# Opening of an encoder layer: the fourth chunk's low weight part moved from a transfer to VectorE, two casts placed later

## The chip, the cores and the metric

One Trainium2 chip, one of its cores. The metric is the device time of one execution in microseconds (us), the median over the runs. The engines are called by their short names in the rows: PE is TensorE (PEld its weight loads), DVE is VectorE, ACT is ScalarE, POOL is GpSimd, and SP is the queue from which most transfers are issued.

## The reference

The kernel computes one layer of a bidirectional encoder on 512 tokens with 1024 channels, in float32. Three sub-layers add to the residual stream: a SwiGLU feed-forward, a mixer of two attentions, and a second SwiGLU. Each begins with an RMS norm that is modulated by a shift and a scale, and these come from a conditioning vector:

```python
c_act = jax.nn.silu(c)
mod = c_act @ w_mod[l] + b_mod[l]
(sh1, sc1, g1, sh2, sc2, g2, sh3, sc3, g3) = jnp.split(mod, N_MOD, axis=-1)
h = modulate(rmsnorm(x, norm_ffn1[l]), sh1, sc1)       # h * (1 + scale) + shift
x = x + 0.5 * g1[:, None, :] * swiglu(h, w_ffn1_in[l], w_ffn1_out[l])
```

Only the start of the first SwiGLU, `h @ w_ffn1_in` for the first four column pairs, matters here.

## The kernel before

Float32 products are made from rounded parts. A number is written as `high + low`, where `high` is the value rounded to the format `float32r` and `low` is the rest. A product is the sum of three matmuls: high by high, high by low and low by high.

The opening computes the first 1024 columns of `h @ w_ffn1_in` (four gate and four up blocks of 128). It goes through the 1024 channels in eight **chunks** `k` of 128. All eight accumulators (`out1`) stay in PSUM, and each chunk adds 24 matmuls of 512 columns: eight of `wh` by `hh[k]`, eight of `wh` by `hl[k]`, eight of `wl` by `hh[k]`. For chunk 7 they are grouped by two accumulators, so `wl` is used after the first four matmuls there. Matmuls of a chunk can't begin before that chunk's `hh` and `wh` are made.

For each chunk this is prepared:

- **Transfers** (`first_loads`): 512 KB of `w_mod` for the scale (`SC1`), 512 KB of the weights (`w1s` into a `raw` tile), 512 KB of `w_mod` for the shift (`SH1`). SP issues them in this order, three chunks ahead; from chunk 3 on each waits until the older tile in its buffer is used up.
- **Scale and shift** (`mod_col`, L282): DVE reduces each 128x1024 tile of `w_mod` against the conditioning vector to a column. For the scale a short ACT instruction (L291) finishes the column.
- **Scaling** (`scaled`, L680): DVE multiplies the chunk of `x` by the inverse root, one 128x512 instruction, made a chunk ahead.
- **Rounding** (`first_high`): ACT applies scale and shift with output `hh[k]` rounded (L692, 128x512), and again unrounded in two halves (L695). DVE subtracts these (`low()`, L699, two halves) to get `hl[k]`.
- **Weights' high part**: ACT casts `raw` to `high` (L668, "the cast").
- **Weights' low part**: for the chunks not in `BY_DMA`, DVE subtracts `raw - high` (`first_low`, L674). For the chunks in `BY_DMA`, ACT writes `low = -raw` rounded (L666), and a GpSimd transfer adds the exact weights from memory to it (L667): what is left is weight minus rounded weight. This transfer reads the same 512 KB again.

The high and low weight parts go round five buffer slots, and `raw` has five buffers. In this part of the program each engine runs its instructions in the order in which the code writes them (`manual_schedule`), so a waiting instruction holds up all that stands behind it on its engine. The order is set by the loop over `k` below: in turn `k` come `first_high(k)`, the cast of chunk `k+1`, for a `BY_DMA` chunk the preparation of chunk `k+2`, the loads of `k+3`, and the DVE work.

After the opening the rest of the layer follows on PE without any other change between the two programs.

Of the kernel before, what the change touches and what calls it, by code (L numbers as in the profile page):

```python
# [14 lines left out]
AF = mybir.ActivationFunctionType  # L15
ALU = mybir.AluOpType
# [104 lines left out]

LAST = 2

BY_DMA = (3, 5, 7)

TO_MIX = (4, 13, 2, 2, 4, 2, 1)
TO_FFN2 = (3, 1, 2, 2, 3, 2, 1)
# [6 lines left out]
def layer(ctx: ExitStack, tc: tile.TileContext, a: dict):  # L134
    nc = tc.nc
    V, S, G, PE = nc.vector, nc.scalar, nc.gpsimd, nc.tensor
# [32 lines left out]
    def f(ap):  # L169
        return ap.bitcast(F32)  # L170
# [25 lines left out]
    def high_low(n=1024, aside=0, holder=None):  # L196
        while turn[0] % HILO in holders:
            turn[0] += 1
        i = turn[0] % HILO
        turn[0] += 1  # L200
        if holder:
            holders[i] = holder
        i = i * (1024 + GAP) + ASIDE + aside
        return tuple(t[:, i : i + n] for t in parts)
# [41 lines left out]
    def mod_load(v, c, w=None, n=1):  # L246
        if w is None:
            w = u4(F32).rearrange("p a b -> p (a b)")
        load_by(w, a["w_mod"][v * NC + c], n)
        return w  # L250
# [22 lines left out]
    def mod_col(v, c, w=None, in_order=False, beside=False, n=1):  # L273
        if w is None:
            w = mod_load(v, c)
        t, b = modv[v][:, c : c + 1], mod_begin(v)[:, c : c + 1]
        by = 1.0 if v in norms or v in (SH1, SH2, SH3) else -0.5 if v == G3 and c % 4 < 2 else 0.5
        so_far = 0.0 if v in norms else b
        for i in range(n):
            j = slice(i * 1024 // n, (i + 1) * 1024 // n)  # L280
            total = t if i == n - 1 else small(1)
            ins = V.tensor_tensor_reduce(  # L282
                out=w[:, j], in0=w[:, j], in1=cact[0][:, j], scale=by, scalar=so_far, op0=ALU.mult, op1=ALU.add,
                accum_out=total,
            )
            so_far = total
        if in_order:
            tc.keep_in_program_order(ins)
        if v in norms:
            if beside:  # L290
                S.activation(t, t, AF.Identity, bias=b, scale=par[:, norms[v] + c : norms[v] + c + 1])  # L291
            else:
                V.scalar_tensor_tensor(t, t, par[:, norms[v] + c : norms[v] + c + 1], b, ALU.mult, ALU.add)
# [332 lines left out]
    with tc.manual_schedule(engines=BOUND | {mybir.EngineType.SP, mybir.EngineType.Pool}):  # L626
# [22 lines left out]
        w1, kept = {}, []  # L649

        def first_loads(k):
            n = 1 if k else 2
            scale = mod_load(SC1, k, n=n)
            if k == 0:
                kept.append(keep([P, 2 * NC], "pos", I32)[:, 0:NT])
            shift = mod_load(SH1, k, n=n) if k == 0 else None
            raw = sbuf("raw", [P, 1024], F32, RAW)
            load_by(raw, a["w1s"][k], n)
            w1[k] = [scale, shift or mod_load(SH1, k), raw]

        def first_split(k):

            raw = w1[k][2]
            hi, lo = high_low()
            if k in BY_DMA:
                S.activation(lo, raw, AF.Identity, scale=-1.0)  # L666
                G.dma_start(lo, a["w1s"][k], accum_op=ALU.add)  # L667
            S.copy(hi, raw)  # L668
            w1[k] += [hi, lo]

        def first_low(k):
            raw, hi, lo = w1[k][2:]
            if k not in BY_DMA:
                V.tensor_tensor(lo, raw, f(hi), ALU.subtract)  # L674

        def scaled(k, rb=None, r=FULL[0]):
            if k not in scaled_x:
                scaled_x[k] = f2()
            rb = spread_sb if rb is None else rb
            V.tensor_tensor(scaled_x[k][:, r], x[k][:, r], rb, ALU.mult)  # L680

        def first_high(k, parts=FULL, between=lambda r: None):

            t = scaled_x.pop(k)
            if k % 4 == 0:
                values = b8(F32).rearrange("p a b -> p (a b)")
                for i in range(2):
                    hq[f"b{k // 4 + 1}{i + 1}"] = values[:, i * 1024 : (i + 1) * 1024]
            v = [hq[f"b{k // 4 + 1}{n + 1}"][:, k % 4 * H : (k % 4 + 1) * H] for n in range(2)]
            by = {"bias": modv[SH1][:, k : k + 1], "scale": modv[SC1][:, k : k + 1]}  # L690
            for r in parts:
                S.activation(hh[k][:, r], t[:, r], AF.Identity, **by)  # L692
                between(r)
            for u, r in zip(v, HALVES):
                S.activation(u, t[:, r], AF.Identity, **by)  # L695

            def low():
                for u, r in zip(v, HALVES):
                    V.tensor_tensor(hl[k][:, r], u, f(hh[k][:, r]), ALU.subtract)  # L699

            return low

        def first_products(k, outs, w, h, r, first, last):
            for i in outs:
                PE.matmul(
                    out1[i][:, r], w[:, i * P : (i + 1) * P], h[:, r],
                    start=first and r.start == 0, stop=last and r.stop == T, skip_group_check=True,
                )
# [60 lines left out]
        raw = w1[0][2]  # L769
# [25 lines left out]
        low()  # L795
        scaled(1)
        first_split(1)
        out1 += [bank("op"), bank("tp")]
        first_products(0, range(6, 8), wh, hh[0], FULL[0], True, False)
# [5 lines left out]
        for k in range(1, NC):  # L805
            low = first_high(k)
            if k + 1 < NC:
                if k + 1 not in BY_DMA:
                    first_split(k + 1)
                if k + 2 in BY_DMA:  # L810
                    first_split(k + 2)
                if k + 3 < NC:
                    first_loads(k + 3)
                scaled(k + 1)
                if k in BY_DMA:
                    mod_col(SC1, k + 1, w1[k + 1][0], beside=True)
                first_low(k)
                low()
                if k not in BY_DMA:
                    mod_col(SC1, k + 1, w1[k + 1][0], beside=True)  # L820
                mod_col(SH1, k + 1, w1[k + 1][1])
            else:
                low()
                first_low(k)
            wh, wl = w1.pop(k)[3:]
            groups = [range(2 * i, 2 * i + 2) for i in range(4)] if k == NC - 1 else [every]
            for outs in groups:
                for w, h in ((wh, hh[k]), (wh, hl[k]), (wl, hh[k])):
                    first_products(k, outs, w, h, FULL[0], False, k == NC - 1 and w is wl)
# [253 lines left out]
    for i in range(2):  # L1083
# [3 lines left out]
            scale=1.0, scalar=0.0, op0=ALU.mult, op1=ALU.add, accum_out=lam_s[:, i : i + 1],  # L1087
# [1021 lines left out]
```

## Time and profile before

| what | value |
|---|---|
| median of 3 runs | 1037.63 us (1037.6 to 1039.89) |
| the profiled execution | 1036.79 us |
| its span, first to last instruction | 1035.0 us |
| PE busy over the span | 1028.5 us (99%) |
| DVE, ACT, POOL busy | 787.0, 583.8, 163.2 us |
| PE idle in the opening's chunks, 20 to 60 us | 1.3 us, once |
| granted TensorE clock, mean | 0.999 |
| data moved by transfers | 220.92 MB |

In the rows that follow, a timeline row has the start in us from the span's begin, the duration in us, the engine, the line and operation, what is written and read, and in brackets the engine's idle time before it with what ended the wait. A row of the chain of waits has start, duration and the engine and line that the end of the program hung on at that time. A row of instruction groups has busy time, the mean of one in ns, and idle time before them. A row of transfers has the count, the size of each and the us from issue to landing. Lines (L...) are those of the program before.

### The profile page before, as it was taken

The numbers are of one execution on the slowest core, as the hardware profiler recorded it, in microseconds if no ns is written. First come the engines' busy times: TensorE is split into PE (matmuls) and PEld (weight loads), VectorE is DVE, ScalarE is ACT, GpSimd is POOL, SyncE is SP. The second block draws the span as 40 slices with busy tenths as digits, with TensorE's granted clock in tenths as the row PEclk, the third lists the DMA queues.
The fourth block names the chain that finished last, engine by engine and source line by source line (L and its number), as shares of the span: only waits on it lengthen the run. The fifth ranks groups of instructions, "written<-read, shape, count | busy, mean of one in ns | idle before, by whom it ended". The sixth has DMA issues, their size and how long they took to land.

```text
span 1035.0 us, 18850 instructions
## 1 busy us (share of the span) xinstructions
PE 1028.5 (99%) x7346; PEld 949.4 (92%) x7346; DVE 787.0 (76%) x1456; ACT 583.8 (56%) x1014; POOL 163.2 (16%) x190
## 2 busy tenths in 40 slices
PE   9999999999999999999999999999999999999998
PEld 7789899899998998899888888989999999999998
DVE  7787667567797679859772598976899777877877
ACT  6664335244365343668785856525867546654553
POOL 1101110110110100543333101001112112112210
PEclk9999999999999999999999999999999999999999
DMA  9977887966884459796737944974498998999974
GB/s 359 359 239 203 233 231 214 255 167 209 250 204 137 149 197 410 242 285 136 187 74 189 252 138 154 363 255 101 92 238 194 237 227 219 221 227 216 209 156 112
DMA packets 70377, 220.92 MB, mean 213 GB/s; under 512 B 8464, under 2 KB 13200, under 8 KB 70288
## 3 DMA queue, kind: packets, MB, share of 16 engines
q1 hardware_dynamic: 47808, 146.52, 39.2%
q0 software_dynamic: 19344, 68.70, 36.1%
q10 hardware_dynamic: 3136, 4.51, 1.2%
q8 instruction: 57, 0.93, 0.3%
q14 instruction: 32, 0.26, 0.1%
HBM read 209.46 MB, written 10.23 MB: 212 GB/s over the span
## 4 chain that ended last, share of the span: by engine, by line
PE 95%; DMA 2%; DVE 1%; ACT 1%; issue 0%; SPq 0%; DVEq 0%; ACTq 0%
PE acc L458 7%; PE acc L457 7%; PE acc L459 7%; PE sc L459 6%; PE sc L458 6%; PE sc L457 6%; PE sc L173 5%; PE sc L174 5%; PE sc L175 5%; PE acc L173 5%; PE acc L175 5%; PE acc L174 5%; PE tp L1277 2%; PE sc L186 2%; DMA raw<-w1s 2%; PE acc L1198 2%
## 5 line engine op out<-in xcount | busy, mean ns | idle before, releaser
L189 ACT CAST high<-raw 128x1024 fp32r<-128x1024 f32 (+2 forms) x176 | 158.4, 914 | 152.2 <-PE sc L174 44.7
L189 DVE TENSOR_TENSOR low<-raw,high 128x1024 fp32r<-128x1024 f32 (+2 forms) x176 | 183.1, 1050 | 41.2 <-ACT high L189 36.6
L457 PE MATMUL acc<-b,high 128*128 128x256 f32 x508 | 140.8, 277 | 0.0
L458 PE MATMUL acc<-b,high 128*128 128x256 f32 x508 | 140.6, 277 | 0.1
L459 PE MATMUL acc<-b,low 128*128 128x256 f32 x508 | 140.5, 277 | 0.0
L459 PE MATMUL sc<-b,low 128*128 128x256 f32 x500 | 138.2, 276 | 0.0
L457 PE MATMUL sc<-b,high 128*128 128x256 f32 x500 | 138.2, 276 | 0.0
L458 PE MATMUL sc<-b,high 128*128 128x256 f32 x500 | 138.2, 276 | 0.0
L189 ACT CAST high<-u 128x1024 fp32r<-128x1024 f32 (+1 forms) x73 | 75.5, 1034 | 50.6 <-PE sc L174 20.0
L189 DVE TENSOR_TENSOR low<-u,high 128x1024 fp32r<-128x1024 f32 (+1 forms) x73 | 87.6, 1200 | 20.6 <-ACT high L189 19.1
L173 PE MATMUL sc<-b,high 128*128 128x512 f32 (+1 forms) x272 | 97.4, 358 | 0.0
L174 PE MATMUL sc<-b,high 128*128 128x512 f32 (+1 forms) x272 | 97.0, 357 | 0.0
L175 PE MATMUL sc<-b,low 128*128 128x512 f32 (+1 forms) x272 | 97.0, 357 | 0.0
L458 PEld LDWEIGHTS acc<-b,high 128*128 128x128 f32 x508 | 95.5, 188 | 0.4 <-DVE b L1893 0.3
L457 PEld LDWEIGHTS acc<-b,high 128*128 128x128 f32 x508 | 95.4, 188 | 0.3 <-ACT f L535 0.2
L459 PEld LDWEIGHTS acc<-b,low 128*128 128x128 f32 x508 | 95.4, 188 | 0.0
L457 PEld LDWEIGHTS sc<-b,high 128*128 128x128 f32 x500 | 94.0, 188 | 0.0
L458 PEld LDWEIGHTS sc<-b,high 128*128 128x128 f32 x500 | 93.9, 188 | 0.0
L459 PEld LDWEIGHTS sc<-b,low 128*128 128x128 f32 x500 | 93.9, 188 | 0.0
L173 PE MATMUL acc<-b,high 128*128 128x512 f32 (+1 forms) x240 | 89.1, 371 | 0.0
L175 PE MATMUL acc<-b,low 128*128 128x512 f32 (+1 forms) x240 | 86.5, 360 | 0.0
L174 PE MATMUL acc<-b,high 128*128 128x512 f32 (+1 forms) x240 | 86.5, 360 | 0.0
(397 smaller groups left out, 2715.6 us busy)
## 6 DMA issues: line engine op xcount, KB each, us to landing
u<-w_mod SPq DMA_DIRECT2D x38, 512.0 KB, 8.3
b<-w_mod SPq DMA_DIRECT2D x32, 512.0 KB, 5.3
raw<-w2i SPq DMA_DIRECT2D x31, 512.0 KB, 5.6
u<-w2i POOLq DMA_DIRECT2D x31, 512.0 KB, 7.1
raw<-w1u SPq DMA_DIRECT2D x24, 512.0 KB, 5.9
u<-w1u POOLq DMA_DIRECT2D x24, 512.0 KB, 6.9
raw<-w1o SPq DMA_DIRECT2D x24, 384.0 KB, 5.0
raw<-w_gate SPq DMA_DIRECT2D x16, 512.0 KB, 5.2
```

Of the source, the lines that this page charges most:

```text
L173: PE.matmul(out, wh, xh, start=first, stop=False)
L174: PE.matmul(out, wh, xl, start=False, stop=False)
L175: PE.matmul(out, wl, xh, start=False, stop=last)
L186: last = PE.matmul(out, of[j][a], of[j][b], start=i == 0, stop=i == 2).ins
L189: last = S.copy(hi, src), V.tensor_tensor(lo, src, f(hi), ALU.subtract)
L457: PE.matmul(out, wh[:, s], xh, start=first and j == 0, stop=False, skip_group_check=True)
L458: PE.matmul(out, wh[:, s], xl, start=False, stop=False, skip_group_check=True)
L459: PE.matmul(out, wl[:, s], xh, start=False, stop=last and j == 1, skip_group_check=True)
L1198: PE.matmul(out[t][:, 0:n], hh[k][:, ht], wh[:, o : o + n], start=k == 0, stop=False)
L1277: PE.transpose(tp[:, j * P : (j + 1) * P], src, ident)
```

## The change

Chunk 3 leaves `BY_DMA`: its low part is now made by DVE like that of chunks 1, 2, 4 and 6. For the chunks that stay, 5 and 7, the old function is cut in two. `first_minus` (the negated weights and the adding transfer) stays where the whole was, in turn `k-2`; the cast goes to turn `k-1`, as for all other chunks. Since the place of `mod_col(SC1, k + 1)` also hangs on `BY_DMA`, in turn 3 DVE now reduces the scale of chunk 4 after `low()`, not before it.

```diff
-BY_DMA = (3, 5, 7)
+BY_DMA = (5, 7)
...
+        def first_minus(k):
+
+            w1[k] += high_low()
+            raw, _, lo = w1[k][2:]
+            S.activation(lo, raw, AF.Identity, scale=-1.0)
+            G.dma_start(lo, a["w1s"][k], accum_op=ALU.add)
+
         def first_split(k):
 
-            raw = w1[k][2]
-            hi, lo = high_low()
-            if k in BY_DMA:
-                S.activation(lo, raw, AF.Identity, scale=-1.0)
-                G.dma_start(lo, a["w1s"][k], accum_op=ALU.add)
-            S.copy(hi, raw)
-            w1[k] += [hi, lo]
+            if k not in BY_DMA:
+                w1[k] += high_low()
+            S.copy(w1[k][3], w1[k][2])
...
             if k + 1 < NC:
-                if k + 1 not in BY_DMA:
-                    first_split(k + 1)
+                first_split(k + 1)
                 if k + 2 in BY_DMA:
-                    first_split(k + 2)
+                    first_minus(k + 2)
```

How the order on the engines changes is shown at three places. The rows give the line, the operation, what is written and read, and the shape; `raw_151`, `raw_279` and `raw_332`/`raw_334` are the weights of chunks 2, 3 and 5, `b_12_97` and `b_13_98` hold `hh` of chunks 0 to 3 and 4 to 7. The lines of the changed program stand two or three higher from L674 on (L692 is L695 there).

First ACT, around the rounding of chunk 2 (`f_61`), before:

```order
L668 CAST high<-raw_151 128x1024
L666 ACTIVATE low<-raw_279 128x1024
L668 CAST high<-raw_279 128x1024
L291 ACTIVATE mod_89<-mod_89,begin,par 128x1
L692 ACTIVATE b_12_97<-f_61_297,mod_88,mod_89 128x512
L695 ACTIVATE b_45_224<-f_61_297,mod_88,mod_89 128x256 x2
```

and now:

```order
L672 CAST high<-raw_151 128x1024
L291 ACTIVATE mod_89<-mod_89,begin,par 128x1
L695 ACTIVATE b_12_97<-f_61_294,mod_88,mod_89 128x512
L698 ACTIVATE b_45_224<-f_61_294,mod_88,mod_89 128x256 x2
L672 CAST high<-raw_279 128x1024
```

The negation of chunk 3's weights is gone and their cast stands behind chunk 2's scale and rounding.

Second ACT, around the rounding of chunk 4 (`f_69`), where chunk 5's weights are prepared, before:

```order
L666 ACTIVATE low<-raw_334 128x1024
L668 CAST high<-raw_334 128x1024
L291 ACTIVATE mod_89<-mod_89,begin,par 128x1
L692 ACTIVATE b_13_98<-f_69_383,mod_88,mod_89 128x512
L695 ACTIVATE b_70_414<-f_69_383,mod_88,mod_89 128x256 x2
```

and now:

```order
L665 ACTIVATE low<-raw_332 128x1024
L291 ACTIVATE mod_89<-mod_89,begin,par 128x1
L695 ACTIVATE b_13_98<-f_69_380,mod_88,mod_89 128x512
L698 ACTIVATE b_70_412<-f_69_380,mod_88,mod_89 128x256 x2
L672 CAST high<-raw_332 128x1024
```

The negation stays ahead of the rounding, the cast goes behind it. The same holds for chunk 7's weights around the rounding of chunk 6.

Third DVE, in turn 3, before:

```order
L680 TENSOR_TENSOR f_69_383<-x_82,f_44_223 128x512
L282 ISA u_58_291,mod_89<-u_58_291,ka_96 128x1024
L282 ISA mod_89 128x1
L699 TENSOR_TENSOR b_14_99<-b_45_224,b_12_97 128x256 x2
L282 ISA u_60_295,mod_88<-u_60_295,ka_96,par 128x1024
```

and now:

```order
L683 TENSOR_TENSOR f_69_380<-x_82,f_44_223 128x512
L677 TENSOR_TENSOR low<-raw_279,high 128x1024
L702 TENSOR_TENSOR b_14_99<-b_45_224,b_12_97 128x256 x2
L282 ISA u_58_288,mod_89<-u_58_288,ka_96 128x1024
L282 ISA mod_89 128x1
L282 ISA u_60_292,mod_88<-u_60_292,ka_96,par 128x1024
```

One subtraction of 128x1024 is added, and the reduction of chunk 4's scale stands behind chunk 3's `hl`. GpSimd has one adding transfer fewer; PE and SP run the same instructions in the same order.

## The prediction

> **What bounds the kernel now.** I read the page's busy times first, then the waits of PE, then the chain of waits in the opening, then the timelines of PE, ACT and DVE around the place it names, and last the transfers. The busy times and PE's waits from 20 to 60 us:
>
> ```profile
> PE 1028.5 (99%) x7346; PEld 949.4 (92%) x7346; DVE 787.0 (76%) x1456; ACT 583.8 (56%) x1014; POOL 163.2 (16%) x190
> PE acc L705 <- ACT b L692: 1.3, 1, 1.3
> ```
>
> PE fills the span, so only time in which PE stands still can be won without removing matmuls, and the change removes none. In the chunks it stands still once, for 1.3 us, waiting for ACT's rounded chunk. The chain of waits up to that place, then PE's timeline across it:
>
> ```profile
> 13.76 10.60 DMA raw<-w1s
> 24.41 0.94 issue
> 25.36 1.03 ACT high L668
> 26.38 0.30 ACT mod L291
> 26.70 0.82 ACT b L692
> 27.57 0.50 PE acc L705
> ...
> 25.88 0.39 PE L705 MATMUL tp<-b,low 128*128 128x512 f32 x1
> 27.57 0.50 PE L705 MATMUL acc<-b,high 128*128 128x512 f32 x1 [1.30 <-ACT b L692]
> 27.91 0.40 PE L705 MATMUL sc<-b,high 128*128 128x512 f32 x1
> ```
>
> The first matmul of chunk 2 (27.57) hangs on ACT's rounding of chunk 2 (26.70), this on the cast of chunk 3's weights (25.36), and this on the negation ahead of it, which waited for the landing of those weights. The next ACT rows show that wait, and DVE's say when chunk 2's own inputs were there:
>
> ```profile
> 24.39 1.06 ACT L666 ACTIVATE low<-raw 128x1024 fp32r<-128x1024 f32 x1 [2.02 <-DMA raw<-w1s]
> ...
> 24.21 0.07 DVE L282 DVE_READ_ACCUMULATOR2_ANT mod<- 128x1 f32 x1
> 24.82 1.21 DVE L674 TENSOR_TENSOR low<-raw,high 128x1024 fp32r<-128x1024 f32 x1
> 28.04 0.92 DVE L699 TENSOR_TENSOR b<-b,b 128x256 fp32r<-128x256 f32 x2 [2.02 <-ACT b L695]
> ```
>
> The shift of chunk 2, the last input of its rounding, was ready at 24.28. So ACT rounded 2.4 us late, held up by work for the chunk after.
>
> **Part 1: chunk 3's negation and cast leave the front of the queue.** ACT then begins chunk 2's rounding at about 24.28 + 0.09 = 24.37 (0.09 is an estimate of the hand-over; from ACT to PE it is 26.70 + 0.82 to 27.57, 0.05) and ends it 0.82 later, at 25.2. PE's last matmul of chunk 1 starts at 25.88 and the rows are 0.23 apart, so chunk 2 would begin at 26.11 with its weight load one pitch before, at 25.9. The rounding is 0.7 us early: the wait is gone altogether. The gain is read at the second matmul, since the first one after the wait was also longer: without a wait it starts at 25.88 + 2 x 0.23 = 26.34, against 27.91. **Gain: 1.57 us**, made of the 1.3 of idle time and 0.27 of restart.
>
> **Part 2: what chunk 3 now costs.** The cast (1.03) moves behind L695 of chunk 2, to about 26.1; its weights landed at 24.36, and PE wants it at 31.6 (a chunk is 24 x 0.227 = 5.44 us). It costs nothing there. The subtraction joins DVE's turn 3. A full turn on DVE, from the groups between 20 and 60 us:
>
> ```profile
> L282 DVE CUSTOM_DVE_ANT_0 u<-u,ka,par 128x1024 f32<-128x1024 f32 x6 | 7.7, 1277 | 0.0
> L282 DVE CUSTOM_DVE_ANT_0 u<-u,ka 128x1024 f32<-128x1024 f32 x6 | 7.3, 1217 | 0.0
> L699 DVE TENSOR_TENSOR b<-b,b 128x256 fp32r<-128x256 f32 x14 | 5.7, 421 | 6.7 <-ACT b L695 6.4
> L674 DVE TENSOR_TENSOR low<-raw,high 128x1024 fp32r<-128x1024 f32 x4 | 4.8, 1212 | 0.0
> L680 DVE TENSOR_TENSOR f<-x,f 128x512 f32<-128x512 f32 x6 | 4.1, 683 | 0.0
> ```
>
> 1.277 + 1.217 + 2 x 0.421 + 1.212 + 0.683 = 5.23 us, under PE's 5.44. DVE also no longer stands 2.02 us before 28.04. Laying the rows end to end from 24.82 (instructions overlap by some 0.07): chunk 2's `hl` at 26.7, chunk 3's scale 27.9 and shift 29.1, `low` of chunk 3 at 30.8, its `hl` 31.6, chunk 4's scale 32.7 and shift 33.9. ACT rounds chunk 3 by 30.0 (wanted 31.4) and, if nothing else holds it, chunk 4 by 34.8 (wanted 36.8). PE wants the `low` at 31.57 + 3.6 = 35.2. **Cost: 0**, hidden behind PE's matmuls of chunks 2 and 3, with 1.4 us or more to spare at each point; without that cover it would be 1.21 us.
>
> **Part 3: the casts of chunks 5 and 7.** The negation still stands ahead of the rounding of chunks 4 and 6, and still waits for its weights:
>
> ```profile
> 34.56 1.06 ACT L666 ACTIVATE low<-raw 128x1024 fp32r<-128x1024 f32 x1 [0.42 <-DMA raw<-w1s]
> 36.88 0.82 ACT L692 ACTIVATE b<-f,mod,mod 128x512 fp32r<-128x512 f32 x1
> 38.58 0.39 PE L705 MATMUL acc<-b,high 128*128 128x512 f32 x1
> 44.62 1.06 ACT L666 ACTIVATE low<-raw 128x1024 fp32r<-128x1024 f32 x1 [0.30 <-DMA raw<-w1s]
> 46.94 0.82 ACT L692 ACTIVATE b<-f,mod,mod 128x512 fp32r<-128x512 f32 x1
> 49.46 0.39 PE L705 MATMUL acc<-b,high 128*128 128x512 f32 x1
> ```
>
> Before, chunk 4 was rounded by 37.70 and wanted one pitch ahead of 38.58, at 38.35. Now it is wanted 1.57 earlier, at 36.78. With the cast behind it, the rounding ends 0.93 earlier (the cast's 1.03 less some 0.1 by which ACT's instructions overlap, as 24.39 + 1.06 does the cast at 25.36), at 36.77, even if the weights landed no sooner. So this move by itself just holds the gain at chunk 4: left out, 0.9 of the 1.57 could be lost there. For chunk 6 likewise 47.76 - 0.93 = 46.83 against 49.23 - 1.57 = 47.66. Cost 0; the casts have 5 us of slack behind.
>
> **Part 4: the transfers.** One adding transfer of 512 KB is gone. What it took from the others is seen in two stretches of 5.5 us (the last two figures are the transfer engines' busy share and GB/s):
>
> ```profile
> 27.60:33.10 5.50, 5.50 (x24) 4.58 (x25) 4.99 (x10) 2.99 (x6) 0.00 (x0) 1.00 1.05 330
> 33.10:38.60 5.50, 5.50 (x26) 4.53 (x26) 3.95 (x7) 5.05 (x8) 0.87 (x1) 1.00 1.02 404
> ```
>
> The transfer engines are full in both. With the adding transfer in flight (27.6 to 33.1; the next is issued only after 35) they move 74 GB/s less, 0.41 MB in 5.5 us or 1.0 us of work; its own 0.52 MB are another 1.3. So all behind it may land up to 2.3 us sooner. Whether that is needed shows at the last user, the `low` of chunk 7 (SP's issue of its scale's tile and of its weights, GpSimd's issue, PE's first use, the landing of the weights, and that of the three adding transfers, of which chunk 7's is the longest):
>
> ```profile
> 33.08 0.33 SPq L244 DMA_DIRECT2D u<-w_mod  x1
> 33.50 0.47 SPq L244 DMA_DIRECT2D raw<-w1s  x1
> 45.98 0.86 POOL L667 DMA_DIRECT2D low<-w1s  x1 [9.19 <-ACT low L666]
> 55.81 0.39 PE L705 MATMUL acc<-b,low 128*128 128x512 f32 x1
> raw<-w1s SPq DMA_DIRECT2D x1, 512.0 KB, 11.0
> DMA to landing us min/median/max: 8.5/8.6/9.0
> ```
>
> The weights land at 44.5, the adding transfer at 45.98 + 9.0 = 54.98, and PE wants it one pitch before 55.81, at 55.58: only 0.6 us to spare, against a gain of 1.57. This is the tight place. Upper bound of the cost: nothing lands sooner, the `low` is 54.98 - 54.01 = 0.97 late, and 0.60 of the gain is left. A middle value: SP issues chunk 7's weights 0.3 earlier and they take the same 11.0 us (the tile issued ahead of them, before at 33.08, waits for the buffer that chunk 4's scale frees, now at 32.7), which leaves 0.9. Lower bound: with 2.3 us less work ahead the weights land at 42.2 and the sum at 52.7, cost 0. The bandwidth rows speak for the last, since a full set of engines with less to do is done sooner; I take **0** and keep 0.97.
>
> The Trainium skill (DMA: Bandwidth & Descriptors, Anatomy of one DMA — SWDGE (gpsimd) path) gives a GpSimd transfer about 2.0 us plus its bytes at 436 GB/s, an estimate of 3.2 us for 512 KB. By it chunk 7's `low` would be there before 50 in any case and the bound of 0.97 would fall away; the row's 9.0 us, beside a full SP queue, decides against using it here.
>
> **Sum and carrying over.** 1.57 + 0 + 0 + 0 = 1.57 us out of the profiled execution: span 1035.0 to 1033.4, its time 1036.79 to 1035.2. The median stands 0.84 above that execution, so 1037.63 - 1.57 = **1036.1**. Behind the opening PE must also be fed 1.57 us earlier. It is busy without a break there, and nothing has an absolute clock: transfers start on buffers that DVE, ACT and PE free, all of which shift along.
>
> ```profile
> 60.00:80.00 20.00, 20.00 (x90) 16.58 (x89) 19.05 (x29) 12.15 (x19) 1.76 (x2) 1.00 0.63 180
> 80.00:100.00 20.00, 20.00 (x168) 19.60 (x168) 15.03 (x17) 10.84 (x14) 3.54 (x4) 1.00 0.84 204
> 87.30 1.05 ACT L189 CAST high<-raw 128x1024 fp32r<-128x1024 f32 x1 [1.60 <-DMA raw<-w1u]
> ```
>
> **The rivals.**
>
> *Chunk 7 eats part of it.* As worked out, between 0.60 and 0.9 is left: 1036.7 to 1037.0. For it: 0.6 us to spare. Against it: the emptier transfer engines.
>
> *The gain is lost behind the opening.* DVE is 95% busy from 60 to 80, and ACT waits 1.60 us for a transfer at 87.30. If such a transfer does not shift, PE gets an idle gap of up to 1.57 and the time is 1037.6. Against it: the transfer share is 0.63 and 0.84 there, so a transfer asked for earlier can run earlier.
>
> *Slower: the last adding transfer falls behind the transfers that SP now issues sooner.* Place: chunk 7's `low`, GpSimd's issue at about 43.7 (weights at 42.2, then 0.12 + 1.36 as in the rows). Price: each us beyond 54.0 - 43.7 = 10.3 to landing stops PE for a us; beyond 11.9 the kernel is slower than before. A plain transfer a little later took longer than that:
>
> ```profile
> raw<-w1u SPq DMA_DIRECT2D x1, 512.0 KB, 13.5
> ```
>
> At 13.5 the stop is 3.2, and the time 1037.63 + 3.2 - 1.57 = 1039.3. Against it: the three adding transfers took 8.5 to 9.0 beside full transfer engines, and SP's list has not grown. The Trainium skill (DMA: Bandwidth & Descriptors, Queues, rings and completion order) says that each transfer engine takes packets in turn from the queues that have work; by that a longer SP queue would not hold GpSimd's transfer up, and this rival would have no chance. The 8.5 to 9.0 agree, but no run here shows it for a longer queue.
>
> *The change doesn't do what it says.* Chunk 2 would still wait: then its shift, not the cast, is the last input. By the DVE row it is there at 24.28, 1.6 us before PE's need, so time stays 1037.6 only if the negation's wait goes to another instruction ahead of the rounding; the new order has none.
>
> **How the numbers follow.** Forecast 0.70 (own range 1035.4 to 1036.8), chunk 7 partly 0.13, lost behind 0.11, slower 0.03, no effect 0.03. A measurement can tell about 0.3%, 3.1 us, from no change. All cases but the far end of the slower one lie within that: the whole effect is 0.15%. Same 0.94; slower 0.02 (a landing over 15 us); faster 0.04, only from the scatter of the runs, which spread by 2.3 us before. Range 1035.0 to 1038.0: it takes in the forecast, both bounds of chunk 7's cost, the lost gain and a few tenths of scatter at each side.
>
> **What would show it.** Step 1: PE's wait before the first matmul of chunk 2 is gone and this starts at 26.1; the chain of waits no longer passes the landing of chunk 3's weights. Step 2: chunk 3's rounding ends near 30.0, no PE wait at 31.6. Step 3: chunk 4's rounding ends by 36.8 and PE starts it at 37.0. Step 4: chunk 7's weights land near 42 and its `low` before 54.0; at 60 us of before PE stands at 58.4. I am wrong if PE shows a new wait between 26 and 60, if its gaps after 60 grow by a us, or if the weights of chunk 5 land as late as before.

## The result and the profile after

The change makes the kernel faster by about a quarter of a percent: 1035.88 us median against 1038.6 us for the kernel before, timed beside it (20 runs each). One of the changed kernel's 20 runs took 5342.79 us, for a reason that the record does not show; the ratio of 0.9977, with a 95% interval of 0.9969 to 0.9986, leaves it out, and without it the median is 1035.56. By the ratio the change is worth 2.4 us of 1038.6, between 1.5 and 3.2; the forecast was 1.57 us, to 1036.1. Timed once more beside the kernel before (under "And without the wait?"), the ratio was 0.9968, 0.9956 to 0.9980.

The profiled execution of the changed kernel happens to be a long one, 1038.52 us with a span of 1036.7, longer than the profiled one of before. It is to be read stage by stage. Its page line of busy times, then PE's timeline where chunk 1 ends and chunk 2 begins (start, duration, engine, line, operation):

```profile
PE 1030.0 (99%) x7346; PEld 950.1 (92%) x7346; DVE 788.1 (76%) x1457; ACT 583.5 (56%) x1013; POOL 162.2 (16%) x189
...
26.76 0.39 PE L708 MATMUL op<-b,low 128*128 128x512 f32 x1
26.98 0.39 PE L708 MATMUL tp<-b,low 128*128 128x512 f32 x1
27.21 0.39 PE L708 MATMUL acc<-b,high 128*128 128x512 f32 x1
27.44 0.39 PE L708 MATMUL sc<-b,high 128*128 128x512 f32 x1
```

Chunk 2 begins at 27.21 in the even pitch of 0.23; the wait is gone, and PE has none between the first matmul of chunk 1 and 60 us. ACT's timeline in the same execution:

```profile
25.51 0.82 ACT L695 ACTIVATE b<-f,mod,mod 128x512 fp32r<-128x512 f32 x1 [0.88 <-DVE mod L282]
27.21 1.03 ACT L672 CAST high<-raw 128x1024 fp32r<-128x1024 f32 x1
32.91 1.06 ACT L665 ACTIVATE low<-raw 128x1024 fp32r<-128x1024 f32 x1
35.03 0.82 ACT L695 ACTIVATE b<-f,mod,mod 128x512 fp32r<-128x512 f32 x1 [0.78 <-DVE mod L282]
42.43 1.06 ACT L665 ACTIVATE low<-raw 128x1024 fp32r<-128x1024 f32 x1
43.80 0.82 ACT L695 ACTIVATE b<-f,mod,mod 128x512 fp32r<-128x512 f32 x1
```

The rounding of chunk 2 (25.51) waits for DVE's shift alone and stands ahead of the cast (27.21). The two negations that are left (32.91, 42.43) don't wait for a landing here, since PE began late in this execution. In a second profile of the changed kernel, in which PE began 1.7 us earlier, they wait again, 0.85 us at chunk 5's weights and 1.27 at chunk 7's, and PE does not stand for it:

```profile
32.16 1.06 ACT L665 ACTIVATE low<-raw 128x1024 fp32r<-128x1024 f32 x1 [0.85 <-DMA raw<-w1s]
33.53 0.82 ACT L695 ACTIVATE b<-f,mod,mod 128x512 fp32r<-128x512 f32 x1
```

Chunk 4's rounding ends there at 34.35, and PE wants it at 36.18. Back to the first profile: the transfers, in windows that answer the two shown of before (the last figures are the transfer engines' share and GB/s), and GpSimd's issue for chunk 7, the landing times of the two adding transfers, and PE's first use:

```profile
27.60:33.10 5.50, 5.50 (x25) 4.53 (x25) 5.50 (x10) 3.87 (x7) 0.00 (x0) 1.00 1.03 411
33.10:38.60 5.50, 5.50 (x26) 4.56 (x25) 5.50 (x11) 3.96 (x7) 0.90 (x1) 1.00 0.98 353
43.79 0.87 POOL L666 DMA_DIRECT2D low<-w1s  x1 [8.61 <-ACT mod L291]
DMA to landing us min/median/max: 9.1/9.1/9.2
55.32 0.39 PE L708 MATMUL acc<-b,low 128*128 128x512 f32 x1
```

From 27.6 to 33.1 the rate is 411 GB/s, where it was 330 with the adding transfer in flight. Chunk 7's `low` lands at 43.79 + 9.1 = 52.9 and is wanted at 55.1. In the second profile, with PE early, there is less room: it lands at 43.60 + 9.0 = 52.6 and is wanted at 53.4.

Why this execution is long all the same: PE began late, and one stage far behind the opening ran at a slower pace. The stage, before and after, for the same 46 us (the first number in brackets counts PE's matmuls):

```profile
762.00:808.00 46.00, 46.00 (x408) 46.00 (x407) 42.91 (x73) 32.56 (x55) 9.09 (x11) 1.00 0.93 216
```

```profile
762.00:808.00 46.00, 46.00 (x393) 45.95 (x392) 41.68 (x70) 31.52 (x53) 9.25 (x11) 1.00 0.90 206
```

In the second, of the changed kernel, PE is busy throughout and has 15 matmuls fewer, at a granted clock of 1.00 in both. In PE's rows from 780 to 783 us the matmuls start 118 ns apart, and 113 ns apart before. That costs 15 x 0.113 = 1.7 us here. Other executions show the slow pace without the change, and the change without the slow pace.

### The profile page after: what moved, and what is told of

Same layout as the page of the kernel before. It is cut to its first block, busy times and chain, and to the rows that moved or that the text cites. A ratio compares the mean times of both kernels' runs of the same rounds, so it can differ in the third digit from the quotient of the medians.

```text
span 1036.7 us, 18849 instructions
## 1 busy us (share of the span) xinstructions
PE 1030.0 (99%) x7346; PEld 950.1 (92%) x7346; DVE 788.1 (76%) x1457; ACT 583.5 (56%) x1013; POOL 162.2 (16%) x189
## 4 chain that ended last, share of the span: by engine, by line
PE 92%; DVE 2%; DMA 2%; ACT 2%; issue 1%; POOL 0%; DVEq 0%; SPq 0%; ACTq 0%
PE acc L457 7%; PE acc L458 7%; PE acc L459 7%; PE sc L459 6%; PE sc L457 6%; PE sc L458 6%; PE sc L174 5%; PE sc L173 5%; PE sc L175 5%; PE acc L173 4%; PE acc L175 4%; PE acc L174 4%; PE tp L1279 2%; PE acc L708 2%; PE acc L1201 2%; PE acc L1200 2%
## 5 line engine op out<-in xcount | busy, mean ns | idle before, releaser
L189 DVE TENSOR_TENSOR low<-u,high 128x1024 fp32r<-128x1024 f32 (+1 forms) x73 | 87.7, 1201 | 21.6 <-ACT high L189 19.9
```

What stands on the lines that cost most here:

```text
L189: last = S.copy(hi, src), V.tensor_tensor(lo, src, f(hi), ALU.subtract)
```

## The experiments

So that neither the late start nor that stage spoils the reading, the opening is measured as a **stretch**: from PE's first matmul of chunk 1 to its first matmul behind the opening. It is 39.85 us in the profiled execution of before (20.49 to 60.34) and 38.24 after (21.61 to 59.85), 1.61 less. All the profiled executions together, times in us:

| kernel | chunk 1 begins | chunk 2 begins | opening ends | stretch | rest of the span |
|---|---|---|---|---|---|
| before | 20.49 | 27.57 | 60.34 | 39.85 | 974.7 |
| before, second profile | 19.90 | 27.61 | 60.39 | 40.50 | 976.1 |
| before, late start | 20.94 | 27.47 | 60.25 | 39.30 | 976.7 |
| changed | 21.61 | 27.21 | 59.85 | 38.24 | 976.9 |
| changed, second profile | 19.92 | 25.53 | 58.17 | 38.25 | 974.7 |
| changed, late start | 21.28 | 26.87 | 59.51 | 38.23 | 974.7 |
| chunk 3 alone | 19.92 | 25.53 | 58.17 | 38.25 | 974.5 |
| casts alone | 20.00 | 26.72 | 59.78 | 39.78 | 974.4 |
| negation kept | 20.37 | 26.72 | 59.49 | 39.11 | 975.3 |
| transfer kept | 20.27 | 25.84 | 59.84 | 39.58 | 976.3 |
| all by VectorE | 20.36 | 25.93 | 58.57 | 38.21 | 974.9 |

The theory was that ACT's wait for chunk 3's weights, in front of chunk 2's rounding, is all that the change takes away. The rivals: that the removed transfer is what counts, and that the moved casts are needed.

### Chunk 3 by VectorE, the casts where they were

The kernel before with

```diff
-BY_DMA = (3, 5, 7)
+BY_DMA = (5, 7)
```

> Chunk 3's low part by VectorE, but the casts of chunks 5 and 7 left ahead of the rounding of chunks 4 and 6. Measure: the stretch from PE's first matmul of chunk 1 to its first matmul behind the opening, 39.85 us before and 38.24 after. Theory A (only the negation that waited for chunk 3's weights cost time; the casts' move is insurance): no PE wait in the chunks, stretch 38.2 to 38.3, total like the changed kernel. Rival B (the moved casts are needed, as the prediction's part 3 held possible): chunk 4's rounding comes up to 0.9 late, PE waits there, stretch 38.5 to 39.2.

Measured: 1035.24 us, ratio 0.9971 (0.9960 to 0.9983), stretch 38.25, no wait of PE. ACT's rounding of chunk 4 with the cast in front of it:

```profile
32.28 1.06 ACT L666 ACTIVATE low<-raw 128x1024 fp32r<-128x1024 f32 x1 [0.97 <-DMA raw<-w1s]
33.25 1.03 ACT L668 CAST high<-raw 128x1024 fp32r<-128x1024 f32 x1
34.60 0.82 ACT L692 ACTIVATE b<-f,mod,mod 128x512 fp32r<-128x512 f32 x1
36.41 0.39 PE L705 MATMUL acc<-b,high 128*128 128x512 f32 x1
```

It ends at 35.42 and is wanted at 36.18, one pitch ahead of 36.41. The whole gain is there without the second half of the change. The weights of chunk 5 landed by 32.2 (before at 34.4), so the cast had room. Rival B falls for this kernel.

### The casts moved, chunk 3 by transfer

The changed kernel with

```diff
-BY_DMA = (5, 7)
+BY_DMA = (3, 5, 7)
```

> Chunk 3's low part by transfer as before; only the casts of chunks 3, 5 and 7 stand behind the next rounding. Theory A: the negation still waits for chunk 3's weights until about 24.4, but the cast (0.93) no longer stands between it and chunk 2's rounding, so PE's wait shrinks from 1.3 to about 0.4 and the stretch is 38.9 (0.93 less than before). Rival C (the removed transfer brings the gain, not ACT's order): stretch stays near 39.8. In both the total lies between the two kernels, about 1 us under before.

Measured: 1036.55 us, ratio 0.9986 (0.9977 to 0.9995). The rounding of chunk 2 moved up by the cast, as theory A says, from 26.70 to 25.85, and chunk 2 begins at 26.72, 0.85 before the 27.57 of before:

```profile
24.48 1.06 ACT L665 ACTIVATE low<-raw 128x1024 fp32r<-128x1024 f32 x1 [2.61 <-DMA raw<-w1s]
25.85 0.81 ACT L695 ACTIVATE b<-f,mod,mod 128x512 fp32r<-128x512 f32 x1
26.72 0.50 PE L708 MATMUL acc<-b,high 128*128 128x512 f32 x1 [0.98 <-ACT b L695]
```

But PE's idle time is 0.98 and the stretch 39.78, not the 0.4 and 38.9 that A expected. The stretch is the number that C gave, though not for C's reason, since the rounding did move. PE began chunk 1 at 20.00 here, 0.49 earlier than in the first profile of before, and the wait grew by that. This was the first sign that its end stands fixed. Another 0.3 went in chunk 7 (54.05 to 59.78, 5.73 for 5.44), whose `low` landed at 55.0, when it was wanted at 54.7: the tight place of the prediction's part 4.

### The negation put back, without a transfer

The changed kernel, in turn 1 with chunk 3's negation on ACT; VectorE overwrites its output.

```diff
+        def first_wait(k):
+
+            w1[k] += high_low()
+            raw, _, lo = w1[k][2:]
+            S.activation(lo, raw, AF.Identity, scale=-1.0)
...
-            if k not in BY_DMA:
+            if k not in BY_DMA and k != 3:
...
+                elif k + 2 == 3:
+                    first_wait(k + 2)
```

> The changed kernel, plus the negation of chunk 3's weights on ACT ahead of chunk 2's rounding as before, without the adding transfer (VectorE overwrites what it writes). It puts the wait back alone. Theory A: ACT waits for chunk 3's weights again, rounding of chunk 2 about 0.6 to 0.8 late for PE, PE idle 0.4, stretch 38.9. Rival C (the transfer was the cost): stretch 38.2 as in the changed kernel.

Measured: 1036.14 us, ratio 0.9977 (0.9966 to 0.9987), stretch 39.11, PE idle 0.61 before chunk 2:

```profile
24.48 1.06 ACT L672 ACTIVATE low<-raw 128x1024 fp32r<-128x1024 f32 x1 [2.23 <-DMA raw<-w1s]
25.85 0.81 ACT L701 ACTIVATE b<-f,mod,mod 128x512 fp32r<-128x512 f32 x1
26.72 0.50 PE L714 MATMUL acc<-b,high 128*128 128x512 f32 x1 [0.61 <-ACT b L701]
```

The wait is back with the negation alone, no transfer needed: 0.87 of stretch over the changed kernel's 38.24, where theory A had 0.7. Rival C, that the transfer alone was the cost, falls. The total doesn't tell it from the changed kernel: 0.9 us is within the intervals. Chunk 2 begins at 26.72 to the hundredth as in the experiment above this one (the casts moved), although chunk 1 began 0.37 later.

### The transfer put back, without ACT

The changed kernel, with an adding transfer of chunk 3's weights into chunk 4's still unused slot. What lands there is overwritten and used by nothing.

```diff
-        w1, kept = {}, []
+        w1, kept, ahead = {}, [], {}
+        slot = 4 * (1024 + GAP) + ASIDE
+        G.memset(f(parts[1][:, slot : slot + 1024]), 0.0)
...
+        def first_beside(k):
+
+            w1[k] += high_low()
+            ahead[k + 1] = high_low()
+            G.tensor_tensor(lam_s, w1[k][2][:, 0:2], half[:, 0:2], ALU.add)
+            G.dma_start(ahead[k + 1][1], a["w1s"][k], accum_op=ALU.add)
...
-            if k not in BY_DMA:
-                w1[k] += high_low()
+            if k not in BY_DMA and k != 3:
+                w1[k] += ahead.pop(k, None) or high_low()
...
+                elif k + 2 == 3:
+                    first_beside(k + 2)
```

> The changed kernel, plus an adding transfer of 512 KB that GpSimd issues when chunk 3's weights land, as in the kernel before, but into a buffer slot that is not in use (zeroed by GpSimd at the start; what lands is overwritten by chunk 4's low part and used by nothing). ACT does nothing for it. It tells the removed transfer's own part. Theory A with the prediction's price (1.0 us of lost rate and 1.3 of bytes): chunk 7's weights land some 2 us later than in the changed kernel counted from chunk 1, and the low part of chunk 7 comes 0 to 0.97 late, stretch 38.2 to 39.2. Rival D (transfers had room, the transfer costs nobody anything): landings as in the changed kernel, stretch 38.2.

Measured: 1036.74 us, ratio 0.9987 (0.9977 to 0.9997), stretch 39.58. Chunk 2 begins without a wait, and chunk 7 has the wait instead. GpSimd issues the transfer at 24.67 here, where the kernel before issued it at 25.76. ACT's negations, GpSimd's issue for chunk 7 with its time to landing, and PE:

```profile
34.48 1.06 ACT L667 ACTIVATE low<-raw 128x1024 fp32r<-128x1024 f32 x1 [2.82 <-DMA raw<-w1s]
35.85 0.81 ACT L704 ACTIVATE b<-f,mod,mod 128x512 fp32r<-128x512 f32 x1
44.54 1.06 ACT L667 ACTIVATE low<-raw 128x1024 fp32r<-128x1024 f32 x1 [1.24 <-DMA raw<-w1s]
45.90 0.87 POOL L668 DMA_DIRECT2D low<-w1s  x1 [9.19 <-ACT mod L291]
low<-w1s POOLq DMA_DIRECT2D x1, 512.0 KB, 9.2
55.14 0.50 PE L717 MATMUL acc<-b,low 128*128 128x512 f32 x1 [0.89 <-DMA low<-w1s]
```

The weights of chunks 5 and 7 are there at 34.4 and 44.5 as in the kernel before, not at 32.3 and 42.4 as in the changed one: the adding transfer costs the others 2.1 us, for which the prediction had 2.3. From 27.6 to 33.1 us the transfer engines move 314 GB/s, against 411 in the changed kernel. So chunk 7's `low` lands at 55.1 and PE stands for 0.89. Rival D falls. Taking the negation off ACT would have won little if the transfer had stayed: 1.34 us of the 1.61 in the stretch go again, 1.22 of them at chunk 7 (53.18 to 59.84 for 5.44; 0.89 of it idle time) and 0.14 at chunk 4. Chunk 4's rounding ends at 35.85 + 0.81 = 36.66 for a chunk that begins at 36.72. By these rows a cast in front of it, 0.93 more, would have made PE wait, so here, with the weights late, the moved cast would be needed; no run with the transfer put back and the cast in front shows it.

### Does the end of the wait move with PE?

The kernel before was profiled again, unchanged and with a later start of PE. The delay is two more idle matmuls in front of the second half of the spread root:

```diff
-        warm(2, 2)
+        warm(4, 2)
```

> The kernel before, looked at once more, since in the looks at the other kernels PE began chunk 1 at 19.9 to 20.4 us and not at 20.5. Theory E (the wait of before ends with the landing of chunk 3's weights, which the transfer engines set at 24.4 us whenever PE begins): chunk 2 begins at 27.5 to 27.7 again; if chunk 1 begins at 20.0, PE's idle time is 1.8, not 1.3, and the change is worth 2.0 us in such an execution. Rival F (the wait moves along with PE's start and is 1.3 in each execution): chunk 2 begins 7.08 us after chunk 1.

> The kernel before with two more idle matmuls of 128x256 on PE ahead of each... that is, two more in the one place between the two halves of the spread root, which delay the start of the chunks by 0.6 to 0.9 us and compute nothing that is used. Theory E: chunk 2 still begins at 27.5 to 27.7, PE's idle time before it shrinks by the delay, the total is as before. Rival F: chunk 2 and the total are later by the delay.

The second profile of before, then the delayed one, at the start of chunk 1 and around chunk 2:

```profile
19.90 0.50 PE L705 MATMUL acc<-b,high 128*128 128x512 f32 x1
24.43 1.06 ACT L666 ACTIVATE low<-raw 128x1024 fp32r<-128x1024 f32 x1 [2.67 <-DMA raw<-w1s]
27.61 0.50 PE L705 MATMUL acc<-b,high 128*128 128x512 f32 x1 [1.96 <-ACT b L692]
```

```profile
20.94 0.50 PE L705 MATMUL acc<-b,high 128*128 128x512 f32 x1
27.47 0.50 PE L705 MATMUL acc<-b,high 128*128 128x512 f32 x1 [0.80 <-ACT b L692]
```

Chunk 1 began at 19.90 and 20.94, a us apart, and chunk 2 at 27.61 and 27.47. PE's idle time was 1.96 and 0.80. The delayed kernel's time is that of before: 1038.16 us, ratio 0.9997 (0.9987 to 1.0007). That interval still lets in a delay of up to 0.7 us, so it is the rows, more than the time, that decide. Theory E holds, F falls: F had chunk 2 at 26.98 and 28.02. In these three profiles chunk 3's weights land at 24.3 to 24.4, and whatever time PE gains or loses before that, this wait takes or gives back; the opening ends at 60.25 to 60.39 in all three. What sets the landing is argued and not tested: the transfer engines' busy share lies between 0.98 and 1.09 from 5 us on, and in all eleven profiles of the table these weights land at 24.3 to 24.7, although SP issues them anywhere between 12.7 and 14.5. The second profile of before is a single execution.

### And without the wait?

> The changed kernel with the same two more idle matmuls. Theory E: nothing absorbs the delay here, since no wait is left that ends at a fixed time; all chunks, and the total, are later by 0.6 to 0.9 us than in the changed kernel. If chunk 7's low part or chunk 5's weights were the bound instead, part of the delay would be absorbed.

> The changed kernel once more, to see an execution in which PE begins chunk 1 early. Theory E: chunk 2 follows chunk 1 after 5.6 us and the stretch is 38.2 whenever chunk 1 begins; if it begins at 20.0 to 20.4, chunk 2 begins at 25.6 to 26.0, 1.6 to 2.0 before the 27.6 of the kernel before. Total about 2.0 us under before, ratio 0.998. If the gain were the 1.57 of the prediction in each execution, the ratio would be 0.9985.

Delayed, the changed kernel has chunk 1 at 21.28, chunk 2 at 26.87 and the opening's end at 59.51: nothing absorbs the delay, the stretch stays at 38.23. Its ratio is 0.9981 (0.9971 to 0.9992), 1036.36 us, in the direction expected against 0.9977 and 0.9968 without delay, though the intervals overlap. The undelayed profiles begin chunk 1 at 19.92 and 21.61, on either side of the delayed one, so the delay itself is no larger than the scatter of the start; what the rows show is that the stretch is the same for all three starts. The second profile of the undelayed kernel, at chunk 1 and chunk 2:

```profile
19.92 0.50 PE L708 MATMUL acc<-b,high 128*128 128x512 f32 x1
25.31 0.39 PE L708 MATMUL tp<-b,low 128*128 128x512 f32 x1
25.53 0.39 PE L708 MATMUL acc<-b,high 128*128 128x512 f32 x1
```

Chunk 1 began at 19.92, as in the second profile of before (19.90), and chunk 2 at 25.53 against 27.61: **2.08 us** won in the opening when PE starts early. The timed runs give 1035.05 against 1038.62 us, ratio 0.9968 (0.9956 to 0.9980). That leaves out the 0.9985 of a constant 1.57 us, with the expected 0.998 at its edge; the interval of the first timing, 0.9969 to 0.9986, just takes 0.9985 in.

### All chunks by VectorE

```diff
-BY_DMA = (5, 7)
+BY_DMA = ()
```

> The changed kernel with chunks 5 and 7 by VectorE too, so no adding transfer is left in the opening. Theory A: PE has no wait in the chunks already, so nothing is won: stretch from chunk 1 to the end of the opening 38.2, total like the changed kernel. Rival G (VectorE becomes the bound, at 5.23 us of work in each turn against PE's 5.44): waits of PE at chunks 6 or 7, stretch over 38.5. It also tells whether the transfer engines, with 2 times 2.3 us less to do, give anything behind the opening.

Measured: 1034.98 us, ratio 0.9969 (0.9956 to 0.9983), stretch 38.21, no wait of PE in the chunks. Without any adding transfer the opening is as long as with two, and the total can't be told from the changed kernel's 0.9968 and 0.9977. VectorE is no bound with a subtraction in each turn; rival G falls.

## Why the prediction was right, and where it was off

The sign, the place and the mechanism came out as forecast, and the time, 1035.88, is 0.2 us from the 1036.1 that was given. That closeness is luck. The forecast started from 1037.63, the median of three runs; the kernel before measured 1038.6 over 20, from which 1.57 less is 1037.0. A start that was 1.0 us too low and a gain that was 0.8 us too small (1.57 for 2.4 by the ratio) made up for each other. What was mis-sized is the gain of part 1.

**Part 1, chunk 2's wait.** Right in mechanism: with the negation out of the way the rounding waits for DVE's shift alone, and PE has no wait. The forecast of 1.57 us is met in the stretch, which fell by 1.61 from the first profile to the first profile. What was off is the step that took this for the gain of every execution. The wait of before ends with a landing near 24.4, whenever PE begins. So the gain is 27.6 less the time at which chunk 2 can begin, 5.6 after chunk 1, and not a constant. The profiled execution of before was one in which PE began rather late (20.49; the undelayed profiles lie at 19.90 to 20.49 but for one at 21.61). For a start at 20.27, the middle one, the term is 27.6 - 25.87 = 1.7; for 19.9 it is 2.1, and for 21.61 only 0.4. The chain of waits had shown it: it led back from chunk 2 to a transfer issued at 13.76 and not to PE's own work, and I read it for the place of the wait, not for what fixes its end.

**Part 2, VectorE's added subtraction.** Right: chunk 3's rounding came by 31.1, PE began the chunk at 32.65 without a wait, and even a subtraction in every turn costs nothing.

**Part 3, the casts.** Right that they cost nothing; the 0.9 us that could be lost without them is not lost, since the weights of chunk 5 land 2 us sooner. By the rows they would be needed if the transfer stayed.

**Part 4, the transfers.** Right that the cost is 0, and near in size: 2.1 us sooner for 2.3 worked out, chunk 7's weights at 42.4 for 42.2, its `low` at 52.9 for 52.7. It was the tight place: the transfer put back costs 0.89 us of waiting there, for which the bound was 0.97. So the gain needs both halves of what left with chunk 3, the negation and the transfer. The 9 us to landing were used rightly in place of the estimate of 3.2 by the Trainium skill (DMA: Bandwidth & Descriptors, Anatomy of one DMA — SWDGE (gpsimd) path): 9.1 and 9.2 in the changed kernel, beside full transfer engines.

**Rivals.** Chunk 7 did not eat part of the gain and the last adding transfer did not fall behind. Nothing shows the gain lost behind the opening: the rest of the span is 974.7 to 976.7 us for the kernel before and 974.7 to 976.9 for the changed one. That scatter would hide a loss of a us, but the timed gain is no smaller than the opening's.

**What stays open.** The opening accounts for 1.7 us at the middle start and 2.1 at the earliest; the timed runs give 2.4 (1.5 to 3.2) and 3.3 (2.1 to 4.6). When PE began in the timed runs that were not profiled is not on record. Whether something behind the opening adds to it can't be said, since the rest of the span varies by 2.5 us between executions of either kind. The stage near 762 to 808 us makes much of that: the slow pace of 118 ns a matmul was seen in the first profile of the changed kernel, in the kernel with the transfer kept and in the delayed one of before, and in none of the other eight profiles (403 to 409 matmuls in the 46 us). What sets it off was not found.

## What to carry to other kernels

When an engine with its work in a fixed order prepares the next chunk's data ahead of the current one's, it makes the current chunk wait for the next chunk's landing; look at what stands in front of the instruction that the bound engine waits for. Ask whether that wait's end is set by the bound engine or by something that runs on its own, such as transfers at full rate: in the second case, the wait's length in one profile is a sample, and other changes in front of it show no effect until it is gone (here PE's start moved by a us and the end of the opening by 0.14). And where removing a wait shifts everything behind it earlier, check each later landing against its new due time; here the next one had 0.6 us to spare for a gain of 1.6.

## What was not expected of the hardware

Chunk 3's weights landed at 24.3 to 24.7 us in every profile, though PE began chunk 1 anywhere between 19.9 and 21.6 and SP issued them between 12.7 and 14.5. One stage of one program ran at a matmul pace of 113 or 118 ns, at a granted clock of 1.00 in both: in the two profiles of the changed kernel PE did 406 and 393 matmuls there in 46 us, 1.5 us of difference.
